# A mixture of 32 experts in plain float32, four experts side by side in the columns of TensorE

## The chip, the cores and the metric

The kernel runs on one core of one Trainium2 chip. The metric is the device time of one execution in microseconds (us); lower is better.

## The reference, cut to what matters

The program is a stack of two blocks on 256 tokens of 1024 numbers, all in float32. The first block is an attention and recurrence mixer, then a mixture of experts; the second block is four layers, each of a feed-forward part, a mixer and a second feed-forward part. Only the mixture of experts changes here:

```python
group_p = softmax(t @ w_group + b_group)             # 4 groups
g_w, g_idx = top_k(group_p, 1)                       # a token takes one group
e_w, e_idx = top_k(softmax(inner logits of it), 2)   # and two of its eight experts
for g in range(4):
    hg = silu(t @ w_gate[g, e]) * (t @ w_up[g, e])   # [256 tokens, 8 experts, 256]
    y = y + einsum(hg * combine[:, g, :, None], w_down[g])
```

(The lines on the router are shortened.) There are 4 x 8 = 32 experts. Each has w_gate and w_up of [1024, 256] and w_down of [256, 1024], so three arrays of 1 MiB in float32 (1.0486 MB), 96 in all. 256 tokens with two experts each make 512 pairs, 16 on the mean for an expert.

## The kernel before, in words

**Places of 8 KB.** Weights stream through pools of tiles of [128, 2048] float32, that is 8 KB on each of the 128 partitions, 1 MiB in all. `raw` has three places, `hi` five and `lo` five (lines 91 to 93). The list `self.jobs` holds all loads of the whole program in the order of their use. `prep()` (line 165) takes the next job, asks for a `raw` place and issues the load on the queue of SyncE (SP). It then splits the tile: ScalarE (ACT) rounds it to fp32r into `hi` (line 221), VectorE (DVE) writes the difference into `lo` (line 222), in two pieces each. A `raw` place is free once DVE has read it. `take()` (line 203) hands out the next job and calls `prep()` for `ahead` jobs more. The instructions of each queue run in the order in which they were issued. A load on SP that waits for its place holds up the loads behind it.

**Experts before.** `jobs_moe` (line 796) lists for each expert w_gate and w_up (split, in row pieces of 256 numbers, 1 KB), and w_down of expert pairs, unsplit, in two places `wd` of their own, loaded on the queue of GpSimd (POOL) in rows of 4 KB (line 177). In `moe` (line 810) the routing comes first: the tokens are normed and turned, `choose` (line 749) picks the experts, and a product with a triangle of ones numbers the tokens of each expert (`place`, line 874). Each expert has 64 places for tokens. `gather(q)` (line 882) builds a one-hot for four experts and multiplies both parts of the tokens with it: `xg` holds the tokens of four experts, transposed, the high and the low part in separate columns. `gate_up` (line 906) has an expert's 64 high and 64 low columns as the stationary operand, and the two parts of its weights stream past, 32 products of 256 columns for an expert (line 913). `hidden` (line 921) turns the result, adds the two parts and makes silu(gate) * up. `down` (line 936) multiplies in plain float32 for two experts side by side, each in 64 columns of the array (line 942). `evacuate` scales and splits the sum, and `scatter` (line 975) adds it to the 256 tokens with the transposed one-hot. Such a pair is one turn of the loop of lines 994 to 1033, 16 in all.

**Overflow.** If an expert has more than 64 tokens, `moe_rest` (line 1042) computes all 32 experts on all tokens for the rest. It stands under `tc.If` at line 1009, behind the last gate products and ahead of the last `down`. Every engine passes that branch.

**Order.** Inside `moe` the order of TensorE (PE) is written out by hand; the other engines are ordered by the planner, with a high priority for evictions. After the experts come `add_to_x` (line 320), `final_norm` (line 1082) and the first feed-forward layer, whose first products are those of line 354.

Of the kernel before, what the change touches and what calls it, by code (L numbers as in the profile page):

```python
# [8 lines left out]
F32 = mybir.dt.float32  # L9
# [10 lines left out]
NT = 2  # L20
# [6 lines left out]
def host_constants():  # L27
    """Tables that depend on shapes alone, one [128, n] array: {name: (first column, shape)}."""
# [46 lines left out]
class Banks:  # L75
    """Four PSUM banks, as one ring or as two rings by turns."""
# [9 lines left out]
class Build:  # L86
    def __init__(self, ctx, tc, io):
# [11 lines left out]
        self.ahead, self.wd_p = 2, None  # L99
# [27 lines left out]
    def load_cols(self, specs, tag):  # L127
        """Vectors of n*128 elements as columns: specs is [(name, ap [r, 128])]; gives {name: (tile, first column)}."""
# [36 lines left out]
    def prep(self):  # L165
        j = self.done
        if j >= len(self.jobs) or (self.jobs[j][2] == "wd" and self.wd_p is None):
            return False
        self.done += 1
        nc = self.nc  # L170
        ap, shape, whole = self.jobs[j]
        if whole == "wd":
            raw = self.wd_p.tile(shape, F32, name="wd", tag="wd", bufs=2)
        else:
            raw = self.raw_p.tile(shape, F32, name="raw", tag="raw")
        if whole == "wd":
            nc.gpsimd.dma_start(out=raw, in_=ap)
        elif isinstance(ap, list):
            for place, a in ap:
                nc.sync.dma_start(out=raw[place], in_=a)  # L180
        else:
            nc.sync.dma_start(out=raw, in_=ap)
# [42 lines left out]
    def rsqrt(self, ms, mul=1.0, eps=EPS):  # L225
        """(mul * (ms + eps)) ** -0.5, elementwise on a small tile."""
# [20 lines left out]
    def factor(self, src, mul=1.0):  # L247
        """(mul * (mean(src ** 2) + eps)) ** -0.5, from the squares of the halves."""
# [53 lines left out]
    def post_norm_add(self, acc, g_row, half):  # L302
        """X += rmsnorm(acc) * g, for each tile of tokens when finish() asks for it"""
# [19 lines left out]
    def finish(self, t):  # L323
        """What is still to be done to the tokens of tile t before they are read"""
# [14 lines left out]
    def mm_t(self, out, w, c0, x, m=128):  # L339
        """out [m features, S] = (x @ w[:, c0:c0+m]).T"""  # L340
# [7 lines left out]
    def mm_tok(self, out, w, x, t):  # L348
        """out [128 tokens, n] = x[token tile t] @ w"""
# [8 lines left out]
    def mm_down(self, acc, w, parts, first, last, tiles=range(NT)):  # L358
        """acc[t] += h @ w for the rows of one job; parts: per 128 rows (hi, lo), each [128, NT, 128]."""
# [17 lines left out]
    def down_by_tile(self, acc, jobs, first):  # L377
        """The last jobs of a sum, [(weights, parts)], for the first tile of tokens and then for the other."""
# [19 lines left out]
    def gate_up(self, g, u, q, x):  # L398
        """One tile of 128 hidden features: silu(x @ g) * (x @ u), transposed, in two parts."""
# [14 lines left out]
    def gate_up_tok(self, g, u, x, t, parts):  # L414
        """Two tiles of 128 hidden features for one tile of tokens."""
# [49 lines left out]
    def log1p_exp_neg_abs(self, z, tmp):  # L465
        """log(1 + exp(-|z|)) by the series of 2 atanh(e / (2 + e)): e / (2 + e) <= 1/3. Left in tmp[3]."""
# [53 lines left out]
    def first_mixer(self):  # L520
        nc, io = self.nc, self.io
        ident = self.c("ident")
        with self.tc.tile_pool(name="m1", bufs=1) as mp:
# [28 lines left out]
            # RG-LRU: convolution and gates  # L552
# [15 lines left out]
            # forget gates: rows are heads  # L568
# [49 lines left out]
            # logits of queries and keys; minus the decay from the start to each key is a bias  # L618
# [60 lines left out]
            # RG-LRU: recurrence  # L679
# [5 lines left out]
            # -expm1(2 y) = -2 t / (1 - t) with t = tanh(y)  # L685
# [29 lines left out]
            self.ahead = 7  # L715
# [16 lines left out]
    def first_of(self, pool, p, m, n, tag):  # L732
        """One-hot of the first element of p [128, n] that equals its maximum m [128, 1]."""
# [25 lines left out]
        # the first group with the largest logit, then the same for its experts, twice  # L759
# [33 lines left out]
    def expert(self, e):  # L793
        return [self.io[n][0, e // 8, e % 8].rearrange("(k p) n -> p k n", p=128) for n in ("w_gate", "w_up", "w_down")]

    def jobs_moe(self):
# [5 lines left out]
                          [128, KD, 36], True))  # L802
        w = [self.expert(e) for e in range(32)]
        for e in range(32):
            self.jobs += [(a, [128, KD, 256], False) for a in w[e][:2]]
            if e >= 2 and e % 2 == 0:
                self.jobs += [(w[i][2], [128, 2, D], "wd") for i in (e - 2, e - 1)]
        self.jobs += [(w[e][2], [128, 2, D], True) for e in (30, 31)]

    def moe(self):  # L810
        """Each expert works on the tokens that chose it, up to 64 of them; if an expert has more, they follow in moe_rest."""
# [9 lines left out]
        self.limit = start  # L821
        self.rw = self.take()
        with self.tc.tile_pool(name="moe", bufs=1) as mp, self.tc.manual_schedule(engines={mybir.EngineType.PE}):
            self.wd_p = mp
# [7 lines left out]
            xT = mp.tile([128, KD, S], F32, name="xT", tag="xs0")  # L832
            with self.tc.high_priority(offset=self.first):
                weights, toks = [], []
                for t in range(NT):
                    self.finish(t)
                    # x * gain; the rest of the norm, a factor for each token, comes later
                    xn = self.wk.tile([128, D], F32, name="xn", tag="xn", bufs=2)
                    for q in range(2):
# [6 lines left out]
                        xT_ins = nc.scalar.activation(out=xT[:, 4 * q:4 * q + 4, 128 * t:128 * t + 128], in_=pt, func=AF.Copy)  # L846
# [5 lines left out]
                    nc.scalar.activation(out=xh[:, t, :], in_=xn, func=AF.Copy, scale=rs)  # L852
                    if t == 1:
                        with self.behind([last]):
                            for i in range(NT):
                                xn, rs = toks[i]
                                tokl_ins = nc.vector.scalar_tensor_tensor(out=xl[:, i, :], in0=xn, scalar=rs, in1=xh[:, i, :].bitcast(F32),
# [3 lines left out]
                    if t == 0:  # L861
                        self.limit = start + 3
                        while self.done <= self.limit and self.prep():
                            pass
# [10 lines left out]
                placed = nc.vector.tensor_scalar(out=place, in0=place, scalar1=-1.0, scalar2=None, op0=OP.add)  # L875
            self.limit = math.inf
            for i in range(4, 6):
                self.after[start + i] = [placed, xT_ins]
            iota = self.c("iota")
            hot, xg = {}, {}  # L880

            def gather(q):
                """hot: 1 where a token has a place with one of four experts; xg: their tokens, transposed, both parts"""
                m = 4
                h = mp.tile([128, NT, m, 64], F32R, name="hot", tag="hot", bufs=2)
                self.hot_ins = nc.vector.tensor_tensor(out=h, in0=iota.unsqueeze(1).unsqueeze(1).to_broadcast([128, NT, m, 64]),
                                        in1=place[:, :, 4 * q:4 * q + m].unsqueeze(3).to_broadcast([128, NT, m, 64]),
                                        op=OP.is_equal)
                hot[q] = h
                for k in range(KD):  # L890
                    p = self.ps.tile([128, 2, m, 64], F32, name="pga", tag="ps")
                    for i, x in enumerate((xh, xl)):
                        for t in range(NT):
# [1154 lines left out]
```

## Time and profile before

| | us |
|---|---|
| median of 3 runs | 2663.9 |
| lowest, highest | 2660.52, 2664.52 |
| span of the profiled execution, first to last instruction | 2659.1 |

The profile records no other time of its execution than this span; the median of the runs lies 4.8 us above it (launch and end).

| engine | busy us | share of the span |
|---|---|---|
| PE (matmul) | 2555.1 | 96% |
| PEld (loading of the stationary operand) | 2327.3 | 88% |
| DVE | 1634.9 | 61% |
| ACT | 1353.5 | 51% |
| POOL | 179.2 | 7% |

The experts lie between about 120 and 452 us of the span. How to read it: matmuls are pipelined, so a busy PE is not a PE at its peak; the share of the DMA engines and the granted clock of TensorE stand in slices of the span.

### The profile page before, as it was taken

What the parts mean: (1) busy time and instruction counts of PE and PEld (TensorE: products, weight loads), DVE (VectorE), ACT (ScalarE), POOL (GpSimd) and SP (SyncE); (2) the same over time, 40 slices, a digit from 0 to 9 for tenths busy, and PEclk for the clock granted to TensorE, in tenths of its full rate; (3) what the DMA queues carried; (4) which work ended last, traced back from release to release, by engine and by line L of the source; (5) the groups of instructions that cost most, each with busy time, mean ns of one, the idle gap of its engine ahead of it and who ended that gap; (6) DMA issues with size and microseconds to landing.
All of it is one profiled execution on the core that took longest, in us unless ns stands there. A gap on an engine that the chain in (4) does not pass through costs nothing.

```text
span 2659.1 us, 44039 instructions
## 1 busy us (share of the span) xinstructions
PE 2555.1 (96%) x18341; PEld 2327.3 (88%) x18341; DVE 1634.9 (61%) x2404; ACT 1353.5 (51%) x2155; POOL 179.2 (7%) x275
## 2 busy tenths in 40 slices
PE   8989998999999999999999999999999999999998
PEld 7767776999989999988779999989989999998998
DVE  7877776555865465567875465465564555576553
ACT  5566665444754454466454454444454454466442
POOL 0100001000120000002000000011110000003000
PEclk9989998999999999999999999999999999999999
DMA  8479996655545555542246555554555555564552
GB/s 254 120 255 350 347 336 229 213 189 164 183 151 197 190 190 189 175 151 66 89 163 202 190 190 188 180 198 148 179 177 183 184 191 190 161 198 144 185 184 83
DMA packets 386598, 502.34 MB, mean 189 GB/s; under 512 B 24736, under 2 KB 344408, under 8 KB 386392
## 3 DMA queue, kind: packets, MB, share of 16 engines
q1 hardware_dynamic: 370032, 449.82, 51.9%
q0 software_dynamic: 8160, 31.46, 3.1%
q10 hardware_dynamic: 8200, 18.19, 2.0%
q8 instruction: 145, 2.38, 0.4%
q14 instruction: 61, 0.50, 0.1%
HBM read 498.38 MB, written 1.05 MB: 188 GB/s over the span
## 4 chain that ended last, share of the span: by engine, by line
PE 65%; issue 10%; DVE 5%; ACT 2%; POOL 1%; DMA 0%; ACTq 0%; DVEq 0%; POOLq 0%
PE gu L345 27%; PE acc L366 18%; PE gut L354 5%; PE pv L354 3%; PE prk L345 2%; PE pu L345 2%; PE pqk L345 2%; PE pg L354 2%; PE po L354 1%; DVE lo L222 1%; PE pt L290 1%; ACT junk L255 1%; POOL rs_r L257 1%; DVE xn L285 0%; ACT hi L221 0%
## 5 line engine op out<-in xcount | busy, mean ns | idle before, releaser
L222 DVE TENSOR_TENSOR lo<-raw,hi 128x1024 fp32r<-128x1024 f32 x842 | 1003.3, 1217 | 514.0 <-ACT hi L221 509.7
L221 ACT ACTIVATE hi<-raw 128x1024 fp32r<-128x1024 f32 x842 | 851.9, 1046 | 429.4 <-PE acc L366 220.2
L345 PE MATMUL gu<-xh,lo 128*128 128x256 f32 x2304 | 322.5, 283 | 0.0
L345 PE MATMUL gu<-xh,hi 128*128 128x256 f32 x2304 | 322.3, 283 | 0.0
L345 PE MATMUL gu<-xl,hi 128*128 128x256 f32 x2304 | 322.1, 283 | 0.0
L345 PEld LDWEIGHTS gu<-xh,hi 128*128 128x128 f32 x2304 | 299.6, 189 | 5.7
L345 PEld LDWEIGHTS gu<-xl,hi 128*128 128x128 f32 x2304 | 295.5, 189 | 0.0
L345 PEld LDWEIGHTS gu<-xh,lo 128*128 128x128 f32 x2304 | 294.8, 189 | 0.0
L406 ACT ACTIVATE sg<-gu 128x256 f32<-128x256 f32 x144 | 55.4, 385 | 336.5 <-PE gu L345 336.4
L366 PE MATMUL acc<-lo,hh 128*128 128x512 f32 x704 | 224.2, 396 | 0.0
L366 PE MATMUL acc<-hi,hl 128*128 128x512 f32 x704 | 221.6, 394 | 0.0
L366 PE MATMUL acc<-hi,hh 128*128 128x512 f32 x704 | 221.1, 395 | 0.0
L408 DVE TENSOR_TENSOR hm<-sg,gu 128x256 f32<-128x256 f32 x144 | 60.2, 418 | 198.0 <-ACT sg L406 197.8
L366 PEld LDWEIGHTS acc<-lo,hh 128*128 128x128 f32 x704 | 132.8, 189 | 30.6
L366 PEld LDWEIGHTS acc<-hi,hl 128*128 128x128 f32 x704 | 132.0, 188 | 30.0
L366 PEld LDWEIGHTS acc<-hi,hh 128*128 128x128 f32 x704 | 127.5, 188 | 23.8
L256 POOL TENSOR_SCALAR rs_a<-ms 128x1 f32<-128x1 f32 x46 | 20.0, 435 | 1655.0 <-ACT junk L255 1633.7
L222 DVE TENSOR_TENSOR hl<-hm,hh 128x256 fp32r<-128x256 f32 x144 | 60.7, 421 | 35.4 <-ACT hh L221 35.4
L221 ACT ACTIVATE hh<-hm 128x256 fp32r<-128x256 f32 x144 | 59.5, 413 | 37.0 <-DVE hm L408 37.0
L354 PE MATMUL gut<-hi,xh 128*128 128x256 f32 x512 | 77.3, 289 | 0.0
L913 PE MATMUL pgu<-hi,xg 128*128 128x256 f32 x512 | 73.8, 285 | 1.7 <-DVE xg L903 1.7
L354 PE MATMUL gut<-lo,xh 128*128 128x256 f32 x512 | 74.7, 287 | 0.0
(530 smaller groups left out, 3648.3 us busy)
## 6 DMA issues: line engine op xcount, KB each, us to landing
raw<-in_ffn_w_gu_dram SPq DMA_DIRECT2D x176, 1024.0 KB, 5.1
raw<-in_ffn_w_down_dram SPq DMA_DIRECT2D x88, 1024.0 KB, 5.0
raw<-in_w_gate_dram SPq DMA_DIRECT2D x32, 1024.0 KB, 8.2
raw<-in_w_up_dram SPq DMA_DIRECT2D x32, 1024.0 KB, 5.8
wd<-in_w_down_dram POOLq DMA_DIRECT2D x30, 1024.0 KB, 8.6
raw<-in_ml_w_in_dram SPq DMA_DIRECT2D x24, 1024.0 KB, 5.3
raw<-in_rt_w_in_dram SPq DMA_DIRECT2D x24, 1024.0 KB, 5.2
row<-in_norm_g_dram ACTq DMA_DIRECT2D x24, 512.0 KB, 4.8
```

What stands on the lines that cost most here:

```text
L221: return (self.nc.scalar.activation(out=hi, in_=src, func=AF.Copy), self.nc.vector.tensor_tensor(out=lo, in0=src, in1=hi.bitcast(F32), op= ...
L222: self.nc.vector.tensor_tensor(out=lo, in0=src, in1=hi.bitcast(F32), op=OP.subtract))
L255: nc.scalar.activation(out=junk[:, qs], in_=src[:, qs], func=AF.Square, scale=mul ** 0.5 / 32.0, accum_out=ms[:, q:q + 1])
L256: nc.gpsimd.tensor_scalar(out=a, in0=ms[:, 0:1], scalar1=ms[:, 1:2], scalar2=mul * EPS, op0=OP.add, op1=OP.add)
L257: nc.gpsimd.tensor_tensor(out=r, in0=a, in1=self.half[:, 0:1], op=OP.pow)
L290: nc.tensor.transpose(out=pt[:, i, :], in_=xn[:, 128 * k:128 * k + 128], identity=self.c("ident"))
L345: nc.tensor.matmul(out=out, lhsT=a[:, k, c0:c0 + m], rhs=b[:, :, k, :], start=(n == 0), stop=(n == 3 * KD - 1))
L354: nc.tensor.matmul(out=out, lhsT=b[:, t, k, :], rhs=a[:, k, :], start=(n == 0), stop=(n == 3 * KD - 1))
L366: self.down_ins.append(nc.tensor.matmul(out=acc[t][:, n, :], lhsT=s[:, t, :], rhs=r[:, q, 512 * n:512 * n + 512], start=(first and q == 0 ...
L406: nc.scalar.activation(out=sg, in_=gu[:, 0, :], func=AF.Silu)
L408: nc.vector.tensor_tensor(out=hm, in0=sg, in1=gu[:, 1, :], op=OP.mult)
L913: nc.tensor.matmul(out=p[:, 256 * i:256 * i + 256], lhsT=xg[k // 4][:, k % 4, e % 4].rearrange("p i s -> p (i s)"), rhs=a[:, k, :], start= ...
```

## The change: what it does

Gate, up and down products use the weights as they are loaded, in float32. No part of the experts' weights is split any more. Loads go straight into any of the 15 places: raw, hi, lo, and two `more`, in a fixed turn that comes round every 15 jobs. All are issued on the SP queue. A row of a partition is now eight rows of the weight array that lie together, 8 KB in one piece; for that the tokens' features are taken in the order that fits (`turned`). w_down keeps its rows of 4 KB. An expert has 32 places instead of 64. `gather` makes one float32 tile for eight experts, the high and low parts added in PSUM. Four experts work side by side, each in 32 columns of the array. There are eight turns of the loop, one for four experts each. The branch for the overflow comes behind the up products of the seventh turn.

```diff
 def prep(self):
+    place = whole if isinstance(whole, str) else "raw"
+    pool = {"raw": self.raw_p, "hi": self.hi_p, "lo": self.lo_p, "more": self.more_p}[place]
...
-        if whole == "wd":
-            nc.gpsimd.dma_start(out=raw, in_=ap)
...
+    def fill(self, upto):
+        while self.done < upto and self.prep():
+            pass
...
 def expert(self, e):
+    return g.rearrange("(p k) n -> p k n", k=KD), u.rearrange("(p k) n -> p k n", k=KD), d.rearrange("(k p) n -> p k n", p=128)
...
 def jobs_moe(self):
+    turn = [h, l, r, r, h, l, h, l, h, l, h, l, m, m, r]
+    where = [turn[i % 15] for i in range(80)] + [h, l, h, l, r, r, r, h, l, h, l, h, m, m, l, h]
+    for q in range(8):
+        for i in range(3):
+            for e in range(4 * q, 4 * q + 4):
+                self.jobs.append((w[e][i], [128, 2, D] if i == 2 else [128, KD, 256], where[n]))
...
 def moe(self):
+    self.ahead = 0
     self.rw = self.take()
+    self.more_p = mp
+    self.fill(start + 15)
...
+    def gather(g):
+        h = mp.tile([128, NT, 8, 32], F32R, name="hot", tag="hot", bufs=2)
+        xg[g] = mp.tile([128, KD, 8, 32], F32, name="xg", tag="xg", bufs=2)
+        for kk in range(4):
+            p = self.ps.tile([128, 2, 256], F32, name="pga", tag="ps")
+            for i in range(2):
+                k = 2 * kk + i
+                for n, x in enumerate((xh, xl)):
+                    for t in range(NT):
+                        nc.tensor.matmul(out=p[:, i], lhsT=x[:, t, 128 * k:128 * k + 128], rhs=h[:, t].rearrange("p e s -> p (e s)"),
+                                         start=(n == 0 and t == 0), stop=(n == 1 and t == 1))
...
+    def used():
+        self.fill(min(self.nxt + 15, end))
+    def project(p, q, i):
+        w = four()
+        for k in range(KD):
+            for e in range(4):
+                nc.tensor.matmul(out=p[32 * e:32 * e + 32, 256 * i:256 * i + 256], lhsT=xg[q // 2][:, k, 4 * (q % 2) + e, :],
+                                 rhs=w[e][:, k, :], start=(k == 0), stop=(k == KD - 1))
+        used()
+    def down(h, c):
+        w = four()
+        for n in range(2):
+            p = self.ps.tile([128, 512], F32, name="pdn", tag="ps")
+            for f in range(2):
+                for e in range(4):
+                    nc.tensor.matmul(out=p[32 * e:32 * e + 32], lhsT=h[:, f, 32 * e:32 * e + 32], rhs=w[e][:, f, ns],
+                                     start=(f == 0), stop=(f == 1))
...
+        used()
...
+    for q in range(8):
+        project(p, q, 0)
+        if z:
+            scatter(q - 1, o, z)
+        project(p, q, 1)
+        o, c = places(q)
+        h = hidden(p)
+        if q == 6:
+            with self.tc.If(some > 32):
+                self.moe_rest(mp, xh, xl, rest)
+        if q % 2 == 0 and q < 6:
+            gather(q // 2 + 1)
+        z = down(h, c)
+    self.ahead = 1
+    self.fill(end + 2)
+    scatter(7, o, z)
```

The rest of the diff removes comments and docstrings and changes nothing else.

## Rows read from the trace of the kernel before

**Rows 1.** The page: its busy line of PE, and the DMA slices.
```profile
PE 2555.1 (96%) x18341; PEld 2327.3 (88%) x18341; DVE 1634.9 (61%) x2404; ACT 1353.5 (51%) x2155; POOL 179.2 (7%) x275
DMA  8479996655545555542246555554555555564552
```

**Rows 2.** Busy time by stretch; the last three columns: granted clock, DMA share, GB/s.
```profile
120.00:150.00 30.00, 21.24 (x103) 18.10 (x102) 21.13 (x65) 14.97 (x24) 4.19 (x6) 0.74 0.58 196
...
234.00:268.00 34.00, 30.67 (x224) 25.72 (x224) 26.14 (x33) 24.58 (x37) 1.51 (x3) 1.00 1.00 343
268.00:302.00 34.00, 31.16 (x229) 26.20 (x224) 25.27 (x36) 23.16 (x35) 2.86 (x4) 1.00 1.04 363
...
440.00:460.00 20.00, 10.06 (x35) 4.93 (x34) 11.92 (x16) 10.73 (x16) 4.80 (x6) 0.79 0.47 161
```

**Rows 3.** Waits of 155 to 440 us: engines, then the SP queue (total, times, longest).
```profile
ACT hi L221 <- DMA raw<-in_w_gate_dram: 22.5, 14, 3.6
...
SPq L182 <- DVE lo L222: 183.5, 41, 7.8
```

**Rows 4.** DMA of 274 to 278 us, when only w_down was moving.
```profile
DMA packets 424, 1.67 MB, mean 418 GB/s; under 512 B 16, under 2 KB 16, under 8 KB 424
q0 software_dynamic: 424, 1.67, 102.5%
```

**Rows 5.** DMA of 334 to 338 us, when only gate and up were moving.
```profile
DMA packets 1371, 1.40 MB, mean 351 GB/s; under 512 B 15, under 2 KB 1370, under 8 KB 1370
q1 hardware_dynamic: 1370, 1.39, 106.9%
```

**Rows 6.** DMA issues of the whole span: KB each, median us to landing.
```profile
raw<-in_ffn_w_down_dram SPq DMA_DIRECT2D x88, 1024.0 KB, 5.0
```

**Rows 7.** Groups by line and shape, whole span: count, busy us, mean ns.
```profile
L913 PE MATMUL pgu<-hi,xg 128*128 128x256 f32 x512 | 73.8, 285 | 1.7 <-DVE xg L903 1.7
L913 PE MATMUL pgu<-lo,xg 128*128 128x256 f32 x512 | 69.9, 279 | 0.0
L942 PE MATMUL pdn<-wd,h 128*64 128x512 f32 x240 | 55.3, 598 | 0.0
L1796 PE MATMUL pY<-SV,AM 32*32 32x32 f32 x128 | 2.6, 203 | 1.4 <-DVE SV L1782 1.4
```

**Rows 8.** The timeline of 200 to 232 us: scatter and down products, loading of their operand.
```profile
213.35 1.17 PE L979 MATMUL acc<-zh,back 128*128 128x512 f32 x4
...
228.70 3.65 PE L942 MATMUL pdn<-wd,h 128*64 128x512 f32 x16
229.18 0.14 PEld L942 LDWEIGHTS pdn<-wd,h 128*64 128x64 f32 x2 [0.28 <-issue]
```

**Rows 9.** The timeline of 122 to 166 us, from the mixer's last product to the first gate product.
```profile
131.07 0.62 PE L366 MATMUL acc<-lo,xh 128*128 128x512 f32 x2
...
131.54 0.63 PE L366 MATMUL acc<-hi,xl 128*128 128x512 f32 x2
...
148.29 0.68 DVE L886 TENSOR_TENSOR hot<-c_iota,place 128x512 fp32r<-128x512 f32 x1
...
149.12 0.77 PE L894 MATMUL pga<-hot,tokh 128*128 128x256 f32 x2 [2.37 <-DVE l L782]
...
155.44 1.24 PE L913 MATMUL pgu<-hi,xg 128*128 128x256 f32 x8
```

**Rows 10.** The timeline of 418 to 475 us: the end of the experts and the next layer.
```profile
444.36 5.35 PE L942 MATMUL pdn<-raw,h 128*64 128x512 f32 x16 [2.55 <-DVEq L1009]
...
450.47 0.75 DVE L971 SCALAR_TENSOR_TENSOR zl<-pdn,cw,zh 128x512 fp32r<-128x512 f32 x1 [1.27 <-ACT zh L970]
...
451.96 2.36 DVE L320 TENSOR_TENSOR X<-acc,X 128x1024 f32<-128x1024 f32 x2 [0.73 <-PE acc L979]
...
461.19 2.08 PE L354 MATMUL gut<-hi,xh 128*128 128x256 f32 x8
```

**Rows 11.** Line 1009, the branch: duration in ns, first and last start in us.
```profile
L1009 SPq EVENT_SEMAPHORE  x8: 17/17/17, 438.3 to 439.0; - x8
L1009 PEldq COMPARE_BRANCH  x1: 3712/3712/3712, 438.7 to 438.7; - x1
```

More of the change, by code (lines that the diff above doesn't have):

```diff
@@ L166, in prep @@
         j = self.done
-        if j >= len(self.jobs) or (self.jobs[j][2] == "wd" and self.wd_p is None):
+        if j >= len(self.jobs):
+            return False
+        nc = self.nc
+        ap, shape, whole = self.jobs[j]
+        place = whole if isinstance(whole, str) else "raw"
+        pool = {"raw": self.raw_p, "hi": self.hi_p, "lo": self.lo_p, "more": self.more_p}[place]
+        if pool is None:
             return False
         self.done += 1
-        nc = self.nc
-        ap, shape, whole = self.jobs[j]
-        if whole == "wd":
[L173 to L176, printed above, removed]
-            nc.gpsimd.dma_start(out=raw, in_=ap)
-        elif isinstance(ap, list):
-            for place, a in ap:
-                nc.sync.dma_start(out=raw[place], in_=a)
+        raw = pool.tile(shape, F32, name="raw" if place == "raw" else "wx", tag=place, **({"bufs": 2} if place == "more" else {}))
+        if isinstance(ap, list):
+            for part, a in ap:
+                nc.sync.dma_start(out=raw[part], in_=a)
         else:
@@ L714, in first_mixer @@
             self.hold()
-            self.ahead = 7
+            self.limit += 4
+            self.ahead = 8
             w = [self.take() for _ in range(4)]
@@ L793, in expert @@
     def expert(self, e):
[L794 removed]
+        g, u, d = (self.io[n][0, e // 8, e % 8] for n in ("w_gate", "w_up", "w_down"))
+        return g.rearrange("(p k) n -> p k n", k=KD), u.rearrange("(p k) n -> p k n", k=KD), d.rearrange("(k p) n -> p k n", p=128)
     def jobs_moe(self):
@@ L874, in moe @@
                 nc.vector.scalar_tensor_tensor(out=place, in0=p[:, 0:2, :], scalar=1.0, in1=on, op0=OP.add, op1=OP.mult)
[L875 to L879, printed above, removed]
-            hot, xg = {}, {}
[L882 to L889, printed above, removed]
-                for k in range(KD):
-                    p = self.ps.tile([128, 2, m, 64], F32, name="pga", tag="ps")
-                    for i, x in enumerate((xh, xl)):
-                        for t in range(NT):
-                            nc.tensor.matmul(out=p[:, i], lhsT=x[:, t, 128 * k:128 * k + 128], rhs=h[:, t], start=(t == 0), stop=(t == 1))
-                    if q == 0 and k % 4 == 0:
-                        xg[k // 4] = mp.tile([128, 4, 4, 2, 64], F32R, name="xg", tag=f"xs{k // 4}")
-                    o = xg[k // 4][:, k % 4, 0:m]
-                    src = p.rearrange("p i e s -> p e i s")
-                    with self.tc.high_priority(offset=self.first):
-                        if k % 2:
-                            nc.scalar.activation(out=o, in_=src, func=AF.Copy)
-                        else:
-                            nc.vector.tensor_copy(out=o, in_=src)
-                    yield
@@ L936, in down @@
-            def down(h, wd):
-                ps = [self.ps.tile([128, 512], F32, name="pdn", tag="ps") for _ in range(2)]
-                for n in range(2):
-                    for f in range(2):
-                        for i in range(2):
-                            nc.tensor.matmul(out=ps[n][64 * i:64 * i + 64], lhsT=h[i][:, f, :], rhs=wd[i][:, f, 512 * n:512 * n + 512],
-                                             start=(f == 0), stop=(f == 1))
-                return ps
-            def places(e2):
-                h = hot[e2 // 2]
-                hp = [h[:, t, 2 * (e2 % 2):2 * (e2 % 2) + 2, :].rearrange("p e s -> p (e s)").bitcast(F32) for t in range(NT)]
+                nc.vector.tensor_scalar(out=place, in0=place, scalar1=-1.0, scalar2=None, op0=OP.add)
@@ L950, in places @@
+            def places(q):
+                hp = [hot[q // 2][:, t, 4 * (q % 2):4 * (q % 2) + 4, :].rearrange("p e s -> p (e s)").bitcast(F32) for t in range(NT)]
                 p = self.ps.tile([128, 260], F32, name="ppl", tag="ps")
@@ L979, in scatter @@
+                used()
+                return zh, zl
+            def scatter(q, o, z):
+                for t in range(NT):
+                    for n in range(2):
+                        for i in range(2):
                             nc.tensor.matmul(out=acc[t][:, n, :], lhsT=o[:, 128 * t:128 * t + 128], rhs=z[i][:, 512 * n:512 * n + 512],
-                                             start=(e2 == 0 and i == 0), stop=(e2 == 15 and i == 1))
-            every_k = lambda g: [None for _ in g]
@@ L983, in moe @@
-            every_k(gather(0))
+                                             start=(q == 0 and i == 0), stop=(q == 7 and i == 1))
+            gather(0)
             with self.behind([self.hot_ins]):
```

152 lines of the change are left out of this document (51 added, 101 removed).

## The prediction

> **What bounds the kernel now.** I read the page first. PE is busy for 96% of the span, so the reader may take TensorE for the bound everywhere; but the DMA slices of the same page (66.5 us each) stand at 9 from the fourth to the sixth, about 199 to 399 us, and at 4 to 6 over most of the rest [rows 1]. Those slices are the experts. So I cut that stage into stretches. In the whole stretches the DMA share is 1.00 to 1.04 at 343 and 363 GB/s, and PE is busy for some 31 of 34 us at full clock [rows 2]. Both are near their limits. The waits decide: ACT stands 14 times for a w_gate that has not landed, and the SP queue, which should issue the next load, stands 41 times and 183.5 us in all until DVE has read the last place for a split [rows 3]. The stage is the transfer of 96 loads, fed through three raw places, with TensorE close behind. On both sides of it DMA is not full: share 0.58 while the router runs, 0.47 at the end [rows 2].
>
> **The change part by part.** I carry the sum to one mark, the first product of the next layer, at 461.19 us before [rows 10]; nothing behind it changes.
>
> *Rate of a load.* A load is 1024 KB [rows 6], 1.0486 MB. The trace has no rows of 8 KB. The nearest below are 4 KB, which alone moved at 418 GB/s [rows 4]; rows of 1 KB alone moved at 351 [rows 5]. The share is full in both. The bounds are 351 (no gain) and, above, 418 with nothing lost; I take the 4 KB row as the nearest, less some 3.5% for the joints between loads: 403 GB/s, 2.60 us for a load. At 418 it is 2.51, at 351 2.99. The page "DMA: Bandwidth & Descriptors" of the Trainium skill, section Specifications, speaks against a gain: it gives a limit of HBM of about 358 GB/s for a core. By that a load takes 2.93 us, which is the first rival below; the 418 GB/s of rows 4 stand above that limit, so the trace does not bear it out.
>
> *TensorE.* Before, a gate or up product of 256 columns costs (73.8 + 69.9) / 1024 = 0.14 us with what it shares, and a down step of 512 float32 columns for two experts 3.65 us for 16 records, 0.43 us for two records at a time [rows 7, 8]. So one float32 product is two records, and two column tiles run beside each other. A record of 256 columns takes half of 0.43, 0.215 us. If four tiles run side by side as two do, a gate product of four experts is 8 steps x 2 records x 0.215 = 3.4 us, up the same, down 2 x 2 x 2 x 0.43 = 3.4 us. Scatter: 8 products, 2 x 1.17 = 2.3 us [rows 8]. The gather of eight experts has as many products as that of four before, from 149.12 to 155.44 at mixed clock [rows 9]; half of some 3.7 at full clock is 1.9. Turning and places: some 1.2. Sum per four experts: 13.4 us, and some 3.5 for waiting on silu and evictions: 17 us. The same four experts are 12 loads, 31.2 us. If only two tiles run together, the products double: 10.2 us more, 27 us, still under 31.2. What is late next is then only the load. Issue is no bound: 128 records in 32x32 tiles took 2.6 us, 0.02 us each, and four records in 0.215 us need 0.054 [rows 7]. With TensorE half idle the clock will fall: the slow stretches before show 0.74 to 0.79 [rows 2]. A group of four loads lands every 10.4 us; even at 1.2 GHz its 3.4 us are 6.9, so the cover holds.
>
> *Splits.* 64 x 2 pieces on ACT and DVE go. Both engines had 8 us or more free in 34 [rows 2], so the work itself is worth nothing; what it held were the raw places, and with those the 183.5 us of rows 3. In their place stand 15 places: a load waits for the products of the job 15 before it. These free four places at once, so at least 11 loads (28 us) are on the way when TensorE begins a group; that hides its 17 us.
>
> *Start.* SP's first loads find places as the mixer's weights are done with, the last pair at 132.2 us; two of its products are 0.47 us apart [rows 9], and with 12 products a weight the first of the last four weights is free at 132.2 - 36 x 0.235 = 123.7. The loads stand in order on one queue: four early, then eleven from about 124, 124 + 11 x 2.6 = 153 us, so 15 lie ready. The one-hot comes at 148.29 and the first gate product at 155.44 [rows 9]; the splits in DVE's queue ahead of it go, four evictions instead of eight; I leave it at 155. The product takes 5 us, half of it at low clock: the first four places are free at 160. DMA stands idle for 7 us there.
>
> *Loads.* 81 are left at 160. All but the last: 160 + 2.4 (first landing: 5.0 alone [rows 6] less 2.6) + 80 x 2.60 = 370.4.
>
> *The branch.* It moves from the end to the seventh turn. SP passes it by eight waits, each for a DMA semaphore, 0.7 us in all when everything had landed [rows 11]. In the new place 15 loads are on the way, so I count that SP waits for them all; PE's branch of 3.7 us [rows 11] lies beside that. Only the 96th load is still to be issued, and it waits: 0.7 + 0.4 + 5.0 alone = 6.1: all landed at 376.5. The loads of the next layer stand behind it: places in raw are free since the last gate products, so the first two land by 383 and are split by 388.
>
> *End.* Down of the last four experts, 3.4 us at full and 6.9 at half clock: 5.2. The second eviction, 0.69 + 0.75: 1.4. The rest of the scatter: 1.2. From the sum into X to the first product of the next layer as before, 461.19 - 451.96 = 9.2 [rows 10]. 376.5 + 17.0 = 393.5, which is 67.7 us earlier than 461.19. The splits due by 388 are done before that.
>
> Only its span is known of the profiled execution, 2659.1, against a median of 2663.9; the same 4.8 us lie around it after. 2659.1 - 67.7 + 4.8 = 2596.
>
> **The rivals.** 1. *Wide rows do not help:* 8 KB and 4 KB move on the long run as 1 KB does, since the limit is on the memory's side. For: whole stretches before never pass 363 GB/s. Against: rows 4. 81 x (2.99 - 2.60) = 31.6 us later: 2628. The page's limit of 358 would give 81 x 0.33 = 27 us, 2623.
>
> 2. *Two of four column tiles run together:* TensorE needs 27 us of 31.2. It is felt where it isn't covered, in the first gate product and the last down, some 2 to 5 us each with the clock: 2603. For: no row shows four tiles of 128 rows at once. Against: nothing in rows 8 ties the count to two, and the two loads of an operand there take 0.14 us of every 0.43.
>
> 3. *Slower: the column tiles run one after the other.* All four share the array's rows and the order of the queue. Then gate and up are 2 x 32 x 2 x 0.215 = 27.5 us, down 16 x 2 x 0.43 = 13.8, and with the other 8.9 a turn takes 50 us: 155 + 8 x 50 + 12 = 567, 106 us later than 461: 2770. It decides from (461 - 155 - 12) / 8 = 36.8 us a turn on. Against: in rows 8 two tiles do run together, and the loading of the next operand (0.14 us) begins while products of both are under way. The page "TensorE: Matmul & The Clock Gate" (section Part 3, the mechanism) of the Trainium skill says that a weight load overlaps products in flight only for another row group; four column tiles have the same one, so by it this rival holds, and 0.14 us more for a record. Rows 8 show otherwise for two tiles.
>
> 4. *The overflow runs.* With 32 places in place of 64 the branch may be taken: over 20 us of products for each of 32 experts, over 650 us. The routing, worked out from the reference for its inputs, puts at most 26 tokens with an expert (up to 30 with three other seeds), so it stays out.
>
> **How the numbers follow.** Forecast 0.55, two tiles 0.18, no gain by rows 0.16, one after the other 0.07, overflow 0.01, an unforeseen loss that eats the gain 0.03 (0.02 of it within 0.2%). The forecast's own range: 418 GB/s takes 7 us off and a warmer start and end 5 more, 2584; places handed on late or a cold clock add 14, 2610. With the second and first rival the range is 2582 to 2634; what is left out is the slower cases and a little below. About 0.2%, 5.3 us, is what a measurement can tell from no change: faster 0.89, same 0.02, slower 0.09.
>
> **What would show it.** In the profile after: a DMA share of 1.0 from about 160 to 370 without dips, at 400 GB/s or more (right) or 350 (rival 1); loads of w_gate and w_up on SP waiting for PE and no longer for DVE; a gate group of 64 records in 3.4 us at full clock, or 6.9 (rival 2), or 13.8 (rival 3); PE busy for about half of each turn and granted clock under 1; one gap of DMA at 153 to 160 and one at the branch near 370; the first product of the next layer at 388 to 400. The prediction is wrong if PE is busy throughout the turns, if DMA has gaps in them, or if the next layer starts on weights that are not there.

## The result, and the profile after

The changed kernel takes 2594.56 us (median of 4 runs, 2583.35 to 2596.41) against 2662.21 of the kernel before in the same comparison: a ratio of 0.9736, 95% interval 0.9715 to 0.9758. The forecast was 2596. The bound and the time came out; but three of the forecast's terms were off and cancelled, and one step, the branch, failed.

First the page of the changed kernel, its busy line of PE and its DMA slices (64.9 us each), which answer to [rows 1]:

```profile
PE 2452.4 (95%) x17989; PEld 2192.1 (84%) x17989; DVE 1444.4 (56%) x2176; ACT 1177.2 (45%) x1899; POOL 159.7 (6%) x245
...
DMA  8489986555455555432365556564455555554552
```

The run of nines is one slice shorter; PE is still "busy for 95%", which says as little about the bound as before. The stretches, with granted clock, DMA share and GB/s in the last three columns, answer to [rows 2]:

```profile
150.00:160.00 10.00, 10.00 (x118) 8.00 (x121) 2.71 (x13) 2.48 (x3) 0.00 (x0) 0.80 0.05 8
...
160.00:330.00 170.00, 127.95 (x1194) 63.22 (x1187) 20.42 (x50) 18.73 (x36) 0.00 (x0) 0.88 1.01 415
330.00:340.00 10.00, 3.67 (x20) 1.23 (x15) 1.04 (x5) 1.15 (x3) 0.00 (x0) 0.74 0.64 238
340.00:370.00 30.00, 20.00 (x176) 8.26 (x176) 2.54 (x7) 2.52 (x5) 0.00 (x0) 0.91 1.01 415
```

From 160 to 370 us the transfers run without a break at 415 GB/s (343 and 363 before), but for one hole at 330 to 340; ahead of them, at 150 to 160, nothing moves. PE is busy for 128 of 170 us at a granted clock of 0.88: it has room. Two runs below, with PE busy for 151 and 166 of the same 170 us, show a clock of 0.94 and 1.00. The page "DMA: Bandwidth & Descriptors" of the Trainium skill, section Specifications, gives about 358 GB/s as the limit of HBM for a core; these rows, of one core at work, do not bear that out.

The SP queue's waits from 160 to 345 us (total, times, longest) answer to [rows 3]:

```profile
SPq L181 <- DMA wx<-in_w_down_dram: 31.9, 16, 2.2
SPq L181 <- DMA wx<-in_w_gate_dram: 31.0, 15, 2.1
SPq L1011 <- SPq L1011: 19.5, 6, 7.0
SPq L181 <- PE pgu L929: 14.4, 8, 3.6
```

No wait for DVE is left. The longest sums are waits for earlier loads: SP's loads go round eight semaphores here, and each load stands until the load eight before it has landed (one issued at 182.58 landed at 202.53, and the eighth behind it went out at 203.40). So eight loads are in flight, not the 11 of the forecast, and eight are enough for a full share.

The timeline of PE (start, us, engine, line, product): the first gate product, a group of four experts, the last down group, the first product of the next layer; to be held against [rows 9, 10].

```profile
155.23 0.41 PE L929 MATMUL pgu<-wx,xg 128*32 128x256 f32 x2
155.24 0.41 PE L929 MATMUL pgu<-raw,xg 128*32 128x256 f32 x2
155.47 0.39 PE L929 MATMUL pgu<-wx,xg 128*32 128x256 f32 x2
...
158.71 3.64 PE L929 MATMUL pgu<-wx,xg 128*32 128x256 f32 x64
...
371.19 3.62 PE L974 MATMUL pdn<-wx,hT 128*32 128x512 f32 x26 [1.52 <-DMA wx<-in_w_down_dram]
...
386.89 2.08 PE L358 MATMUL gut<-hi,xh 128*128 128x256 f32 x8
```

Four records start within 0.04 us (two places "wx", two "raw": four experts), and the next four 0.24 us later: four column tiles run side by side, 64 records in 3.64 us. The next layer starts at 386.89 in place of 461.19. Last, the branch on SP (count, ns, first and last start), against [rows 11]:

```profile
L1011 SPq EVENT_SEMAPHORE  x8: 17/17/17, 321.9 to 334.6; - x8
...
L1011 SPq COMPARE_BRANCH  x1: 50/50/50, 314.9 to 314.9; - x1
```

SP reaches the branch at 314.9 and passes its eight waits only at 334.6, when all it has sent has landed. Thirteen loads stand behind. That is the hole.

### The profile page after: what moved, and what is told of

It is laid out like the page before. It is cut to its first block, busy times and chain, and to the rows that moved or that the text cites. A ratio compares the mean times of both kernels' runs of the same rounds, so it can differ in the third digit from the quotient of the medians.

```text
span 2594.3 us, 42603 instructions
## 1 busy us (share of the span) xinstructions
PE 2452.4 (95%) x17989; PEld 2192.1 (84%) x17989; DVE 1444.4 (56%) x2176; ACT 1177.2 (45%) x1899; POOL 159.7 (6%) x245
## 4 chain that ended last, share of the span: by engine, by line
PE 64%; issue 10%; DVE 6%; ACT 3%; DMA 2%; POOL 2%; SPq 0%; ACTq 0%; DVEq 0%; POOLq 0%
PE gu L349 28%; PE acc L370 18%; PE gut L358 4%; PE pv L358 2%; PE prk L349 2%; PE pu L349 2%; PE pg L358 2%; DVE lo L226 2%; PE po L358 1%; PE pqk L349 1%; DMA wx<-in_w_down_dram 1%; POOL rs_r L261 1%; ACT junk L259 1%; ACT hi L225 1%; POOL rs_a L260 1%
## 5 line engine op out<-in xcount | busy, mean ns | idle before, releaser
L226 DVE TENSOR_TENSOR lo<-raw,hi 128x1024 fp32r<-128x1024 f32 x714 | 851.5, 1217 | 463.5 <-ACT hi L225 463.5
L225 ACT ACTIVATE hi<-raw 128x1024 fp32r<-128x1024 f32 x714 | 723.6, 1045 | 394.3 <-PE acc L370 214.4
L929 PE MATMUL pgu<-wx,xg 128*32 128x256 f32 x784 | 84.0, 449 | 29.9 <-DMA wx<-in_w_gate_dram 18.6
L929 PEld LDWEIGHTS pgu<-wx,xg 128*32 128x32 f32 x784 | 37.9, 128 | 72.5 <-DMA wx<-in_w_gate_dram 27.6
```

What stands on the lines that cost most here:

```text
L225: return (self.nc.scalar.activation(out=hi, in_=src, func=AF.Copy), self.nc.vector.tensor_tensor(out=lo, in0=src, in1=hi.bitcast(F32), op= ...
L226: self.nc.vector.tensor_tensor(out=lo, in0=src, in1=hi.bitcast(F32), op=OP.subtract))
L929: nc.tensor.matmul(out=p[32 * e:32 * e + 32, 256 * i:256 * i + 256], lhsT=xg[q // 2][:, k, 4 * (q % 2) + e, :], rhs=w[e][:, k, :], start=( ...
```

## The experiments

Edits are to the changed kernel unless another is named. "The mark" is the first product of the next layer.

Each run has one profile, and profiles of one kernel differ: the changed kernel, profiled twice, comes to its first gather product at 149.14 and at 146.02 us, before any edit acts. So the marks are best compared from a common point. The table takes the first load that SP issues after the standstill at 150 to 159 ("loads go on").

| run (us) | first gather | first gate product | loads go on | mark | loads go on to mark |
|---|---|---|---|---|---|
| changed kernel | 149.14 | 155.23 | 158.90 | 386.89 | 228.0 |
| changed kernel again | 146.02 | 151.52 | 155.19 | 383.19 | 228.0 |
| rows of 1 KB | 143.97 | 150.35 | 154.03 | 410.25 | 256.2 |
| gate and up twice | 146.02 | 151.62 | 158.74 | 387.12 | 228.4 |
| branch's loads on POOL | 149.19 | 155.19 | 158.87 | 383.32 | 224.5 |
| the same again | 146.25 | 152.69 | 156.36 | 380.81 | 224.5 |
| 8 places for 80 loads | 149.67 | 156.12 | 159.79 | 391.93 | 232.1 |
| 8 places for all | 149.73 | 156.12 | 159.79 | 406.50 | 246.7 |
| gather in halves | 149.41 | 156.39 | 162.41 | 390.71 | 228.3 |
| both edits | 146.28 | 153.27 | 158.14 | 384.47 | 226.3 |

The changed kernel needs 228.0 us both times, so in this column differences of a few tenths count.

**Rows of 1 KB again.** What do the long rows alone give?

```diff
-        return g.rearrange("(p k) n -> p k n", k=KD), u.rearrange("(p k) n -> p k n", k=KD), d.rearrange("(k p) n -> p k n", p=128)
+        return g.rearrange("(k p) n -> p k n", p=128), u.rearrange("(k p) n -> p k n", p=128), d.rearrange("(k p) n -> p k n", p=128)
...
-                    nc.scalar.activation(out=by_k(xh[:, t, :]), in_=turned(xn), func=AF.Copy, scale=rs)
+                    nc.scalar.activation(out=xh[:, t, :], in_=xn, func=AF.Copy, scale=rs)
...
```

> The changed kernel with its gate and up weights in rows of 1 KB (features in plain order, so the token copies are not turned); places, order and products as in the changed kernel, w_down stays at 4 KB. Theory, the row length sets the rate of a load: in the stretch from 160 to 370 us the rate falls from 418 to about 370 GB/s, a gate or up load takes 2.99 us in place of 2.50, 54 of the 81 loads are of that kind, so +26 us: 2621 (2614 to 2630). Rival A, rows are worth nothing and the whole gain is the queue without splits: 2594, within 5 us. Rival B, eight times as many pieces hold up the issue of the loads as well: DMA share below 0.95 in the stretch and more than 35 us lost, over 2630.

Measured: 2616.97 us, ratio to before 0.9826 (0.9801 to 0.9852); mark at 410.25, 23.4 us later than with long rows. By the table the transfers take 28.2 us longer, near the 26 of the theory; the first gather comes earlier, by 3 us of the spread just named and by 2 us for token copies that are not turned.

```profile
160.00:330.00 170.00, 122.12 (x1003) 57.04 (x1002) 19.30 (x45) 17.61 (x33) 0.00 (x0) 0.82 1.08 367
```

367 GB/s at a share of 1.08, where the changed kernel has 415 at 1.01. The DMA engines were full both times; short rows are dearer for the same bytes. Half of rival B is there: 54 issues of a load took over 1 us on SP between 150 and 380 us, 190 us in all, where the changed kernel has 22 and 55. It cost nothing, since the share stayed full.

**Long rows in the kernel before.** The same edit the other way round, with the turned token copies, in the kernel before.

> The kernel before with nothing but the 8 KB rows for gate and up (and the turned token copies that go with them); splits, raw places and two column tiles stay. Theory, TensorE and the raw places that wait for splits stand close behind the transfers: PE was busy 31 of 34 us in the whole stretches, so at most 9% of some 250 us, 22 us, can come; I expect 2645 (2638 to 2658). Rival, the rate alone is the change's gain: 64 gate and up loads each 0.5 us shorter, 32 us, and more with the shorter joints: 2630 or less. A third way, slower because the turned copies cost 2 us before the first product: 2664 or more.

Measured: 2655.98 us, ratio 0.9976 (0.9963 to 0.9989): 5 us, near the low end of the expected gain. A stretch of it, and its SP queue from 155 to 440 us:

```profile
234.00:302.00 68.00, 62.91 (x442) 50.59 (x441) 52.78 (x70) 47.04 (x71) 4.29 (x6) 1.00 0.93 348
```
```profile
SPq L182 <- DVE lo L222: 188.0, 40, 7.7
```

DMA now has time over (share 0.93) and moves no more bytes: 348 GB/s. PE is busy for 63 of 68 us and SP stands 188 us for DVE, as in [rows 3]; which of the two holds the transfers, or whether both do, this run does not tell. Long rows are worth 22 us where the queue runs free, and 5 where it is held.

**Nothing side by side.** Rival 3's price.

```diff
-   nc.tensor.matmul(out=p[32 * e:32 * e + 32, 256 * i:256 * i + 256], lhsT=xg[q // 2][:, k, 4 * (q % 2) + e, :],
-                    rhs=w[e][:, k, :], start=(k == 0), stop=(k == KD - 1))
+   nc.tensor.matmul(out=p[:, 256 * i:256 * i + 256], lhsT=xg[q // 2][:, k, 4 * (q % 2):4 * (q % 2) + 4, :].rearrange("p e s -> p (e s)"),
+                    rhs=w[e][:, k, :], start=(k == 0 and e == 0), stop=(k == KD - 1 and e == 3))
...
```

(The down products change in the same way.)

> The changed kernel, but the four experts' products of a step go one after another over the full width of 128 columns and are summed, so that nothing runs side by side (its sums mix the experts). The number of product instructions is the same. Theory, four column tiles really share the 0.215 us: here each of the four takes 0.215 us, gate and up 27.5 us a turn, down 13.8, with the rest some 50 us a turn; PE busy throughout at full clock, end about 2770 (2740 to 2800). Rival, side by side is only how the records look and the products took their turn all along: 2595, within 10 us.

Measured: 2752.0 us (one execution), mark at 550.6. Part of a group, and the stretch that answers to that of the changed kernel:

```profile
202.11 1.03 PE L929 MATMUL pgu<-wx,xg 128*128 128x256 f32 x4
202.98 0.59 PE L929 MATMUL pgu<-raw,xg 128*128 128x256 f32 x2
203.41 1.46 PE L929 MATMUL pgu<-wx,xg 128*128 128x256 f32 x6
...
215.50 0.59 PE L929 MATMUL pgu<-wx,xg 128*128 128x256 f32 x2
215.74 0.58 PE L987 MATMUL acc<-zh,back 128*128 128x512 f32 x1
```
```profile
160.00:330.00 170.00, 166.09 (x711) 127.81 (x711) 12.46 (x32) 11.12 (x22) 0.00 (x0) 1.00 0.64 256
```

Records now follow each other at 0.215 us, and the gate group takes from 202.11 to 215.74, 13.6 us, where 13.75 was forecast for the tiles in turn and 3.64 is what the changed kernel needs. PEld is busy for only 128 of 170 us, so the wider operand's loading does not set this pace. So the four tiles do share their time. In the prediction I let a sentence of "TensorE: Matmul & The Clock Gate" (Trainium skill, section Part 3), by which a weight load overlaps products in flight only for another row group, speak for rival 3. It is a sentence on loads, and these rows of the changed kernel do not bear it out for column tiles, which have one row group:

```profile
158.71 0.82 PE L929 MATMUL pgu<-wx,xg 128*32 128x256 f32 x10
158.71 0.55 PEld L929 LDWEIGHTS pgu<-wx,xg 128*32 128x32 f32 x10
```

Ten loads stand between 158.71 and 159.26 beside ten products of 158.71 to 159.53.

**Gate and up twice.** How well is TensorE covered?

```diff
-                for k in range(KD):
-                    for e in range(4):
+                for _ in range(2):
+                    for k in range(KD):
+                        for e in range(4):
...
```

> The changed kernel with every gate and up product done twice (the second pass writes over the first): 6.9 us more of TensorE for each four experts at full clock. Theory, TensorE is covered: a turn has 30 us of transfers and some 17 us of TensorE, 24 us now; only the first group is felt, whose places come free 3 to 7 us later: 2600 (2595 to 2605). Rival, TensorE's chain of groups is nearly the bound as its waits are counted in: a turn grows by 3 us or more: over 2618, up to 2650.

Measured: 2591.07 us (2588.8 to 2596.74), ratio 0.9737 (0.9711 to 0.9763); mark at 387.12. In the time nothing is to be seen of 16 groups of 3.64 us, 58 us more of TensorE, and the time lies below the expected range; but the table shows the theory's mechanism. The loads went on 7.1 us after the first gate product in place of 3.7 (151.62 to 158.74, 155.23 to 158.90), and from there to the mark it took 228.4 us in place of 228.0. So the first group, doubled, costs some 3.5 us, which this execution hid by reaching it 3.6 us earlier; the other 15 cost 0.4 us together. PE is busy for 151 of the 170 us instead of 128, at a clock of 0.94.

**The branch's loads on POOL.** What holds SP at the branch?

```diff
 def moe_rest(self, mp, xh, xl, rest):
-            nc.sync.dma_start(out=w, in_=ap)
+            nc.gpsimd.dma_start(out=w, in_=ap)
...
-            nc.sync.dma_start(out=w, in_=w_down)
+            nc.gpsimd.dma_start(out=w, in_=w_down)
```

> The changed kernel with the loads inside the overflow branch issued by POOL instead of SP; the order on PE, ACT and DVE stays the same instruction for instruction. Theory, the eight waits at SP's branch exist because the branch's body holds SP's own loads, and they empty the queue: with the loads elsewhere SP passes at once, the DMA share stays at 1.0 through 330 to 340 (0.64 there in the changed kernel), the first product of the next layer comes 4 us earlier (383, from 386.9), and the time is 2590.5 (2587 to 2593), ratio 0.9985 to the changed kernel. Rival A, SP waits at any branch until its loads have landed, whoever issues those inside: same as the changed kernel, 2594.6 within 2. Rival B, POOL's side of the branch costs what SP saves: 2595 to 2600.

Measured: 2584.91 us, ratio 0.9711 (0.9693 to 0.9729); mark at 383.32, 3.6 us earlier. The branch's line and the stretch of the hole:

```profile
L1011 POOLq EVENT_SEMAPHORE  x4: 17/43/43, 151.5 to 151.8; - x4
...
L1011 SPq COMPARE_BRANCH  x1: 50/50/50, 315.0 to 315.0; - x1
```
```profile
330.00:340.00 10.00, 3.55 (x26) 1.59 (x25) 1.04 (x5) 1.15 (x3) 0.00 (x0) 0.74 1.02 411
```

SP keeps the branch and loses the eight waits; they are now POOL's, at 151.8, when it has nothing under way. The hole is gone. So the waits belong to the queue whose loads stand inside the branch, not to the branch. The time fell by 9.7 us where 4 was expected, so both were run again side by side:

> The changed kernel once more, beside the next run on the same chip: 2594 (2590 to 2598).

> The kernel with the branch's loads on POOL once more, beside the changed kernel. If the 9.7 us that lay between the two medians were the drained queue alone, it would be 4; the profile showed 3.6 at the first product of the next layer and 6 less behind it. Theory, the 3.6 and some 1.7 of next-layer weights that come earlier are real and the rest is the spread between executions: 5 us below the run before this one, 2589 (2585 to 2592). Rival, all of it is real: 9 to 10 us below.

Measured: 2593.88 us, as expected (0.9745, 0.973 to 0.976), and 2580.98 us (0.9702, 0.9689 to 0.9716), 12.9 us apart: the rival, and somewhat more. The kernel with the branch's loads on POOL is faster than both kernels of this case. The hole itself is worth 3.5 us by the table, 224.5 in place of 228.0 in both pairs; what lies beyond that is not the hole. In the second pair of profiles 2.4 us lie ahead of the mark (383.2 and 380.8) and 6.7 behind it (2204.7 and 2198.0 us to the end). Most of these 6.7 come with one load, the first w_down of the next layer. In all of these runs SP issues it 6.9 us after the mark, and it lands (the last number, us) after

```profile
raw<-in_ffn_w_down_dram SPq DMA_DIRECT2D x1, 1024.0 KB, 8.0
```

in the changed kernel, 7.9 in its second run, 6.3 and 4.8 in the two runs of this one. Where it takes 4.8 (and 5.1 in the run with both edits below), the layer's product `gu`, 32 us after the mark, is 0.2 (0.4) us later than before; with 6.3 and 6.4, 1.6 and 1.7; with 7.4 to 8.0 in five kernels, 2.7 to 4.7. Before, SP issued it 11.0 us ahead of the mark and its 7.8 us were covered. The load does not run alone: SP issues the next one 2.3 us behind it in all ten profiles of the table. One thing tells the profiles apart. In the six with 7.4 to 8.0 us a packet of 16 KB of the instruction queue, which took 0.88 us, went out 4.3 to 4.7 us after the load; in the four with 4.8 to 6.4 us none fell between its issue and its landing. In the changed kernel, 393 to 400 us:

```profile
q8 instruction: 1, 0.02, 0.8%
```

That this packet delays the load, and that the branch's edit moves it, is not shown: no run changed it alone.

**Eight places instead of 15, twice.** First for the first 80 loads, with the list for the last 16 as it was, then for all 96, which is the edit shown:

```diff
-        turn = [h, l, r, r, h, l, h, l, h, l, h, l, m, m, r]
-        where = [turn[i % 15] for i in range(80)] + [h, l, h, l, r, r, r, h, l, h, l, h, m, m, l, h]
+        turn = [r, h, h, r, h, h, r, h]
+        where = [turn[i % 8] for i in range(96)]
```

> The changed kernel with 8 places in place of 15 for the loads of the first 80 jobs (five of the one pool and the three raw ones, in a ring). Theory, the places buy a head start and not the rate: 8 loads instead of 15 lie ready at 155, so 7 loads of 2.50 us come later, +17.5 us, and inside the turns nothing more, since no more than 8 loads are in flight in the changed kernel either and a group's products take 4 of the 10 us of its four loads: 2612 (2606 to 2618), DMA share still 1.0 from 170 on. Rival A, places hide TensorE's waits in the turns: gaps in every turn, share below 0.9, over 2630. Rival B, places beyond 8 are worth nothing: 2595, within 4.

> As the run with 8 places, but with the ring of 8 for all 96 loads: in that run seven loads of the last two turns had places of their own and SP sent them out first, so that the head start was not taken away. Here 8 loads instead of 15 lie ready when TensorE starts. Theory, the 7 loads missing at the start have to move later at 2.50 us each, and a ring of 8 is enough inside the turns: DMA idle from about 140 to 159, share 1.0 after that, +17.5 us: 2612 (2607 to 2617). Rival A, the head start is worth nothing either, since something else is late: 2595, within 4. Rival B, a ring of 8 leaves gaps in the turns too: over 2620.

Measured: 2594.53 us (0.9742, 0.9723 to 0.976) and 2613.05 us (0.9813, 0.9798 to 0.9828). The first missed by 17 us because it did not take the head start away: loads of the last turns had places of their own, and SP's order put them first, so 14 loads still went out ahead; by the table it lost 4 us to the mark all the same, which the time does not show. The second did, with 8 loads ahead, and came out at the theory's 2612: mark at 406.50, 19.6 us later, 18.7 of it after the loads went on. Its stretches:

```profile
140.00:150.00 10.00, 4.52 (x19) 4.29 (x20) 7.35 (x32) 0.34 (x4) 0.00 (x0) 0.50 0.31 112
160.00:330.00 170.00, 122.39 (x1074) 57.73 (x1068) 18.92 (x48) 17.60 (x35) 0.00 (x0) 0.89 1.01 410
```

In the turns next to nothing is lost with eight places (410 GB/s in place of 415); seven loads that no longer run beside the router are 17.7 of the 18.7 us.

**The first gather in two halves**, alone and with the branch's loads on POOL. The experts 0 to 3 are gathered ahead of the first turn, 4 to 7 in it.

```diff
-                                nc.tensor.matmul(out=p[:, i], lhsT=x[:, t, 128 * k:128 * k + 128], rhs=h[:, t].rearrange("p e s -> p (e s)"),
+                                nc.tensor.matmul(out=p[:, i, 0:32 * n_e], lhsT=x[:, t, 128 * k:128 * k + 128], rhs=h[:, t, half].rearrange("p e s -> p (e s)"),
...
-                if q % 2 == 0 and q < 6:
-                    gather(q // 2 + 1)
+                if q == 0:
+                    gather(0, slice(4, 8))
+                if q in (1, 2, 4):
+                    gather((q + 1) // 2 + (q != 1))
```

> The changed kernel, but the first gather takes the tokens of four experts only and the second half of it follows after the first turn's gate and up products (the next gather moves from the first turn to the second). Theory, the loads stand still from 150 to 159 because all 15 places are full until the first gate group is done, and what stands ahead of that group is 6.1 us of gather: half of it goes, first gate product at 152.3 in place of 155.2, first freed place near 156, the whole stage 2.9 us earlier: 2591.7 (2589 to 2594). Rival, the evictions of the gather or the weights of the places on DVE are late next, or the colder clock eats it: no gain, 2594.6 within 1.5.

> The changed kernel with both edits of the two runs above: the branch's loads on POOL and the first gather in two halves. Theory, the two gaps in the transfers are separate and add: 4 + 2.9 us, first product of the next layer at 380, 2587.6 (2584 to 2591), below the kernel before and the changed one. Rival, TensorE or the next layer's weights take up part of it behind the mark: 2591 or more.

Measured: 2593.23 us (0.9735, 0.9719 to 0.975) and 2589.78 us (0.9722, 0.9705 to 0.9738): no gain, and the second is 4.9 us slower than the branch's edit alone, measured beside it. PE in the first:

```profile
149.41 0.66 PE L914 MATMUL pga<-hot,tokh 128*128 128x128 f32 x2 [1.36 <-DVE l L787]
149.86 0.63 PE L914 MATMUL pga<-hot,tokl 128*128 128x128 f32 x2
150.29 0.63 PE L914 MATMUL pga<-hot,tokh 128*128 128x128 f32 x2
...
156.39 0.64 PE L935 MATMUL pgu<-wx,xg 128*32 128x256 f32 x2
```
```profile
150.00:160.00 10.00, 10.00 (x67) 8.05 (x70) 2.73 (x14) 2.15 (x5) 0.00 (x0) 0.50 0.01 2
```

Two gather products take 0.43 us at half clock with 128 columns, what two of 256 take in the changed kernel at that clock:

```profile
149.70 0.63 PE L908 MATMUL pga<-hot,tokl 128*128 128x256 f32 x2
150.12 0.63 PE L908 MATMUL pga<-hot,tokh 128*128 128x256 f32 x2
```

Half the columns saved nothing, and the first gate product came at 156.39. The granted clock stayed at 0.50 through the whole stretch, where the changed kernel's was 0.80, so the first gate group was slow as well and the loads went on at 162.41 in place of 158.90. The stage lost 3.5 us where 2.9 were to be gained; from there to the mark all is as before (228.3). The rival (the clock eats it) holds for the gate group; the step that failed is that a product's time goes with its columns. With both edits the loads went on 4.9 us after the first gate product in place of 3.7, and the last down group ran at half clock, 5.57 us in place of 3.62, which is the rest: the mark lies 3.7 us behind that of the branch's edit alone (384.47, 380.81), with the first gather at the same time.

## Why the prediction came out

**Bound.** The stage was a transfer held by what followed each load, and is now a transfer: shown by the pair of the first two experiments. That the splits were what held it, and not TensorE, is argued from the waits and not shown. From before to the changed kernel with short rows is 44 us (splits gone, four products side by side, the head start of 15 places), the rows on top of that 22, the rows alone 5.

**Rate.** 2.60 us a load was forecast; 1.0486 MB at 415 GB/s are 2.53. Over 81 loads that is 5.6 us too slow. I took 3.5% off for joints between loads; with eight in flight the rate is 0.7% under the 418 of the bound.

**TensorE.** 3.4 us a group forecast, 3.64 measured; places free at 158.9, not 160; the gap foreseen in the transfers at 153 to 160 stands at 150 to 159. My sum for four experts was wrong: its terms make 15.6 us and not 13.4, which leaves the scatter out, so 19 us with the waits and not 17. That changes nothing, since the cover holds, but for the first group, with 7 us more for each four experts. The turned token copies, which I did not price, take 2.1 us each in place of 1.2. From the mixer's last product to the first gather it is 17.5 us with them (131.65 to 149.14) and 15.8 with plain ones in the run with short rows (128.20 to 143.97): 1.7 us.

**Splits.** "At least 11 loads (28 us) are on the way" was wrong in number (eight) and in reason: 15 places are worth their head start, 18 us, and next to nothing in the turns. The diff also lets `first_mixer` ask for eight jobs ahead in place of seven, and for four more of them, which helps this head start; no run has it apart.

**The branch: the step that failed.** "Only the 96th load is still to be issued, and it waits." Thirteen loads stood behind the branch on SP, which came to it at 314.9 while PE came at 331.5. The price, 3.5 us by the table, is the 3.5 I had put in (6.1 less the load's own 2.6): the queue runs empty once and fills again, but in the middle of the stage and with thirteen loads behind it, not at its end with one. That the sizes agree is luck as far as the place goes.

**The mark.** 393.5 forecast, 386.9 measured: 6.6 us too late, of which the rate is 5.6 and the places' start 1.1. Of the signs that I named, this one failed (388 to 400; the second profile has 383.2), PE was busy for 128 of 170 us and not for half, and the branch's gap stands at 330 and not near 370. It lies inside the turns, which I had named as a sign against me.

**Behind the mark.** "Nothing behind it changes" was wrong: from the mark to the end it took 2197.9 us before and 2207.4 after, 9.5 us given back in that execution (6.8 in the second profile; 1.9 and 0.1 with the branch's loads on POOL). 3.3 of it is the next layer's w_down, issued 18 us later in relation to the mark. The rest comes in later stages, above all 4 us in the RWKV stage. The other runs lose 0 to 4 us there, the kernel before with long rows 3 of them and the changed kernel's second profile 1.4, so I take it for spread between executions; that is argued and not shown.

**Around the span.** I added 4.8 us, the median less one span. The profiled executions themselves have 1.8 (2596.13 - 2594.3; 2584.91 - 2583.1), 3.0 less.

So 2596 came from -6.6, +9.5 and -3.0. The range would have held the time with each of them alone; the agreement to 1.5 us is luck.

**Rivals.** No gain by rows (2628): false, with 415 GB/s; short rows for gate and up cost 22 us in the time; the rival's 31.6 counted all 81 loads, and w_down's rows of 4 KB kept their rate. Two tiles only, and one after the other: false by the timeline; the latter costs 2752 where 2770 was reckoned. The overflow did not run.

## What to carry to other kernels

Compare a stage between the same two points of each profile, since its start alone moved by 3 us between executions of one kernel here. Faster transfers show only once nothing else holds the queue: test the rate alone in the old kernel before counting on it. The branch emptied the queue of the engine that has transfers inside it, so put those on a queue that is idle there. When a stage ends earlier, look at what its neighbour had loaded beside it: that work moves with the mark or past it.

## What the runs showed of the hardware that was not expected

One queue with eight loads in flight held 415 GB/s for 170 us at rows of 8 and 4 KB; with rows of 1 KB in two of three loads it was 367, at a share of 1.08. A gather product took 0.215 us at half clock with 128 as with 256 columns. The granted clock rose from 0.50 at about 154 us in the changed kernel, where PE had been busy without a break since 149.1; with the gather halved it rose at about 161, since 149.4. A load of 1 MB, with the next one issued 2.3 us behind it, landed after 4.8 to 8.0 us in the ten profiles of the table, and after more than 7 only where an instruction packet of 16 KB fell inside it.
